# A decoder layer's FFN input: seven block products in place of eight for 19 of 22 steps

## The chip, the core and the metric

The kernel runs on one core of one Trainium2 chip. The metric is device time in microseconds (us) of one execution. The core has five engines with an instruction stream each, executed in order: PE (TensorE, matmuls; its weight loads appear as PEld), DVE (VectorE), ACT (ScalarE), POOL (GpSimd) and SP (SyncE, which here issues most transfers). They wait for one another through semaphores. On-chip memory is SBUF, with PSUM banks for the results of PE; a bank's tag in this kernel is one letter (g, s, t, d).

## The reference

One decoder layer for a prompt of 512 tokens with 16 meta tokens ahead of it, and for 8 samples of 8 tokens, of the same weights: differential attention and a gated delta rule (GDN) beside each other, their branches merged by gates, an output projection, then the gated FFN. The change concerns the FFN's first half:

```
xn = rmsnorm(x, p['ln_ffn_pre'])
up, gate = jnp.split(xn @ p['w_ffn_in'], 2, axis=-1)
gate, new_ffn_conv = causal_dwconv(gate, ffn_conv_buf, p['ffn_conv_w'], p['ffn_conv_b'])
x = x + rmsnorm((jax.nn.gelu(gate) * up) @ p['w_down'], p['ln_ffn_post'])
```

`xn` has 1024 features; `w_ffn_in` has 2 x 2816 columns; the convolution has width 3 along the tokens. The last two rows of `gate` before the convolution are outputs too (`new_ffn_conv`).

## The kernel before

Activations are held transposed, with features on the 128 partitions and tokens in the free dimension: 578 columns for the FFN (two meta tokens, 512 of the prompt, 64 of the samples). Products keep nearly the precision of float32: every operand is split into a rounded part `hi` (an ACT cast, L305) and the rest `lo` (a DVE subtraction, L306), and a product is three matmuls, hi by hi, hi by lo and lo by hi (L263). Weights come in tiles of 4 x 128 rows by 128 columns (512 elements a partition), loaded by SP into `wraw` (three buffers), two tiles for a column block.

The FFN input (`ffn_in`) walks 22 blocks m of 128 columns. A step makes the gate block g and the up block u: each eight blocks of 128 rows by three matmuls by two halves of the tokens (258 and 320 columns for g, 256 and 320 for u), 96 matmuls in all, in banks taken in turn. g is copied by ACT to `fpre` (L1656 to L1658); POOL puts the state rows ahead of it (L1655) and copies its last two rows to `ftail` (L1660, L1661). The convolution is one DVE tensor_scalar (L1665) and two DVE scalar_tensor_tensor (STT, L1669), each over 592 elements; gelu is on ACT (L1672). DVE multiplies by u out of PSUM (L1675 to L1677), and the product is split at once to `ghi` and `glo` (L1683, L1684) for the second half of the FFN, `ffn_out`. PE transposes `ftail` (L411), DVE copies it to `ftailT` (two buffers, L1688), and POOL's queue stores it (L1690, L1691).

The order of each engine is that of the program, with some reordering by a scheduler. Three half products are issued early (EARLY), since the last block of tokens is late. The convolution's constants and states, `fw`, are loaded by three DMAs on ACT's queue (L1622 to L1624) and transposed by PE in 22 pieces just after the first step's g; DVE copies them out (L1629). Ahead of the FFN stand `mix` and `out_proj`, whose `finish` normalises a block of tokens, transposes it (L411) and splits it into the FFN's input parts. Long before, the stage of the gates (`gate`, whose tanh is L1490) fills PE beside the last GDN head.

## Time and profile before

| | us |
|---|---|
| median of 3 runs | 1219.9 |
| lowest and highest run | 1218.33, 1222.36 |
| the profiled execution | 1219.77 |
| its span, first to last instruction | 1218.0 |
| granted TensorE clock, mean | 0.991 |
| a step of the FFN input (see the prediction) | 12.89 |

The profile is that of one execution. Its page gives the busy time of each engine, the groups of instructions by line of the kernel with their mean duration, and the chain of work that ended last. Other views of the same trace give busy time by stretch of time, the waits, the instructions of one line, and a timeline. In a timeline row the first number is the start, the second the duration, and xN counts instructions joined in a row; in a group's row the numbers after the bar are the busy time in us and the mean of one in ns. PE's matmuls overlap in the pipeline, so the spacing of starts, not the duration of one, is what a matmul costs; the same holds in part for DVE and ACT.

### The profile page before, as it was taken

The page shows a single profiled execution, that of the slowest core. Times are in us where ns is not written, and L with a number is a line of the kernel's source. Part 1 is how long each engine was busy: PE and PEld are TensorE (multiplying, and loading weights), DVE is VectorE, ACT ScalarE, POOL GpSimd, SP SyncE. Part 2 cuts the span into 40 slices and gives each one's busy share as a digit, 9 for nine tenths or more (in the row PEclk, how much of TensorE's full clock was granted, in tenths as well). Part 3 has the DMA queues.
Part 4 walks back from the last instruction along what each step waited for, and adds up shares of the span by engine and source line. Part 5 has one row for each costly group of instructions (what it writes and reads, how often), then busy time and mean ns, then how long its engine had stood idle before and what let it go on. Part 6 is the DMA issues. An engine that isn't in the chain of part 4 may idle for free.

```text
span 1218.0 us, 23729 instructions
## 1 busy us (share of the span) xinstructions
PE 1159.3 (95%) x8927; PEld 1036.0 (85%) x8927; DVE 638.2 (52%) x1719; ACT 447.3 (37%) x1139; POOL 206.5 (17%) x341
## 2 busy tenths in 40 slices
PE   6999999979999989899999999999999999999996
PEld 5977787757687677599998987899999999999996
DVE  5456667596487388346235753455545545422224
ACT  5234445443343243343233433433333333323322
POOL 2122221150241231221010002321111111100000
PEclk9999999999999999999999999999999999999999
DMA  6364525736936946713221552322223223352222
GB/s 197 77 237 133 160 64 180 238 113 201 302 108 192 300 154 192 252 47 86 69 70 55 149 163 87 102 81 85 75 86 88 84 75 88 95 166 79 79 80 85
DMA packets 185002, 157.57 MB, mean 129 GB/s; under 512 B 13234, under 2 KB 147315, under 8 KB 184867
## 3 DMA queue, kind: packets, MB, share of 16 engines
q1 hardware_dynamic: 179569, 147.53, 40.1%
q0 software_dynamic: 4288, 5.16, 1.5%
q10 hardware_dynamic: 1030, 3.35, 0.9%
q8 instruction: 71, 1.16, 0.4%
q14 instruction: 44, 0.36, 0.1%
HBM read 146.12 MB, written 9.88 MB: 128 GB/s over the span
## 4 chain that ended last, share of the span: by engine, by line
PE 69%; issue 13%; DVE 9%; POOL 3%; ACT 3%; DMA 2%; SPq 0%; DVEq 0%; ACTq 0%; POOLq 0%
PE ps_d L263 28%; PE ps_g L263 14%; PE ps_t L263 11%; PE ps_s L263 9%; PE ps_t L411 6%; DVE cy L639 1%; PE ps_m L263 1%; DVE KT L1393 1%; DMA page<-in_cache_k 1%; DMA page<-in_cache_v 1%; DVE vt L646 1%; DVE wlo L306 0%; DVE yn L1744 0%; POOL xr L406 0%; ACT whi L305 0%
## 5 line engine op out<-in xcount | busy, mean ns | idle before, releaser
L306 DVE TENSOR_TENSOR wlo<-wraw,whi 128x512 fp32r<-128x512 f32 x238 | 159.6, 684 | 243.6 <-ACT whi L305 241.9
L305 ACT CAST whi<-wraw 128x512 fp32r<-128x512 f32 x240 | 142.7, 613 | 253.9 <-PE ps_d L263 106.6
L263 PE MATMUL ps_d<-xhi,whi 128*128 128x256 f32 (+2 forms) x704 | 219.0, 311 | 0.0
L263 PE MATMUL ps_d<-xhi,wlo 128*128 128x256 f32 (+2 forms) x704 | 213.5, 304 | 1.2 <-DVE wlo L306 1.2
L263 PE MATMUL ps_d<-xlo,whi 128*128 128x256 f32 (+2 forms) x704 | 213.3, 303 | 0.3 <-DVE xlo L306 0.2
L263 PEld LDWEIGHTS ps_d<-xhi,whi 128*128 128x128 f32 x704 | 134.3, 191 | 7.4 <-issue 4.2
L263 PEld LDWEIGHTS ps_d<-xlo,whi 128*128 128x128 f32 x704 | 134.1, 190 | 3.6 <-issue 2.5
L263 PEld LDWEIGHTS ps_d<-xhi,wlo 128*128 128x128 f32 x704 | 133.8, 190 | 2.6 <-DVE wlo L306 1.6
L411 PE MATMUL ps_t<-consts,page 128*128 128x128 f32 x512 | 73.5, 283 | 8.9 <-DVE KT L1393 7.5
L411 PEld LDWEIGHTS ps_t<-consts,page 128*128 128x128 f32 x512 | 57.5, 143 | 25.5 <-issue 10.3
L263 PE MATMUL ps_t<-fhi,whi 128*128 128x320 f32 (+2 forms) x208 | 62.1, 299 | 0.1
L1393 ACT COPY KT<-ps_t 128x512 f32<-128x512 f32 x64 | 37.4, 585 | 65.5 <-PE ps_t L411 62.8
L263 PE MATMUL ps_t<-flo,whi 128*128 128x320 f32 (+2 forms) x208 | 61.3, 295 | 0.0
L263 PE MATMUL ps_t<-fhi,wlo 128*128 128x320 f32 (+2 forms) x208 | 61.1, 295 | 0.0
L263 PE MATMUL ps_g<-fhi,whi 128*128 128x320 f32 (+2 forms) x200 | 59.5, 298 | 0.0
L263 PE MATMUL ps_g<-flo,whi 128*128 128x320 f32 (+2 forms) x200 | 58.9, 295 | 0.0
L263 PE MATMUL ps_g<-fhi,wlo 128*128 128x320 f32 (+2 forms) x200 | 58.7, 294 | 0.0
L263 PE MATMUL ps_d<-fhi,whi 128*128 128x320 f32 (+2 forms) x192 | 57.4, 299 | 0.2 <-ACT fhi L305 0.2
L263 PE MATMUL ps_d<-flo,whi 128*128 128x320 f32 (+2 forms) x192 | 56.8, 296 | 0.0
L263 PE MATMUL ps_d<-fhi,wlo 128*128 128x320 f32 (+2 forms) x192 | 56.7, 296 | 0.0
L1393 DVE COPY KT<-ps_t 128x512 f32<-128x512 f32 x64 | 43.7, 685 | 18.1 <-PE ps_t L411 17.9
L263 PEld LDWEIGHTS ps_t<-fhi,whi 128*128 128x128 f32 x208 | 39.1, 188 | 0.7 <-ACT whi L305 0.3
(554 smaller groups left out, 2824.6 us busy)
## 6 DMA issues: line engine op xcount, KB each, us to landing
page<-in_cache_k SPq DMA_DIRECT2D x128, 256.0 KB, 4.1
page<-in_cache_v SPq DMA_DIRECT2D x128, 256.0 KB, 4.3
wraw<-in_w_in SPq DMA_DIRECT2D x88, 256.0 KB, 3.4
wraw<-in_w_ffn_in SPq DMA_DIRECT2D x88, 256.0 KB, 3.1
wraw<-in_w_down SPq DMA_DIRECT2D x40, 256.0 KB, 3.0
wraw<-in_w_out SPq DMA_DIRECT2D x16, 256.0 KB, 3.0
x<-in_x_prompt SPq DMA_DIRECT2D x4, 512.0 KB, 7.4
st<-in_state_gdn SPq DMA_DIRECT2D x4, 512.0 KB, 4.1
```

Of the source, the lines that this page charges most:

```text
L263: self.nc.tensor.matmul(out, lhsT, rhs, **kw)
L305: self.nc.scalar.copy(hi, raw)
L306: (eng or self.nc.vector).tensor_tensor(out=lo, in0=raw, in1=hi.bitcast(F32), op=ALU.subtract)
L411: self.nc.tensor.transpose(out, in_, self.ident[:k, :k])
L639: nc.vector.scalar_tensor_tensor(out=y, in0=pre[:, j : j + n], scalar=self.cw[:, ch, 24 + j : 25 + j], in1=y, op0=ALU.mult, op1=ALU.add)
L646: nc.vector.scalar_tensor_tensor(out=dst, in0=part(th), scalar=1.0, in1=part(y_), op0=ALU.add, op1=ALU.mult)
L1393: (nc.scalar.copy if j % 2 else nc.vector.tensor_copy)(kt[:, :, 128 * j : 128 * j + 128], tp)
```

## The change

Steps 0 to 2 stay as they are in kind, with token halves of equal width: the input is now held in four blocks `f["11"]`, `f["12"]`, `f["21"]`, `f["22"]`, the first index for the half of the features, the second for the half of the tokens, of 290 columns each (256 of the prompt, 32 of the samples, 2 for the meta tokens, zero in the second half). Steps 3 to 21 compute g and u together as the product of a 2 x 2 block matrix of weights (a11, a12 the two halves of g's rows; a21, a22 those of u) by the 2 x 2 blocks of f, with seven block products in place of eight (Winograd's form of Strassen's scheme). Each is 12 matmuls of 290 columns:

- weight sums: s1 = a21 + a22, s2 = s1 - a11, s3 = a11 - a21, s4 = a12 - s2. s1 and s3 are made on POOL, s2 and s4 on DVE. Each of s1 to s4 and a22 is split, beside g's two tiles: seven splits a step in place of four.
- input sums t1 to t4, made once by `differences` for each half of the feature blocks: five DVE and five POOL operations and four splits of 580 elements each time, during the plain steps.
- p1 and p2 give g's first half. In bank A (tag g) p1, p6, p7, p4 are accumulated on one another; ACT copies the bank after p1 (for g) and after p6 (`u2`), DVE reads it after p7 (into `p5`) and after p4 (u's first half). In bank C (tag t) p3 is accumulated on p5, after an ACT copy. The order on PE is p1, p5, p2, p6, p4 of the step before, its tail transpose, p3, p7, so that two products lie between a bank's copy and the next product into it.
- g's halves are summed into `fpre` by DVE (`add_g`), the convolution's first operation moves from DVE to ACT (Identity with scale and bias), u's second half is multiplied on POOL, its first half on DVE.
- u's weights have buffers of their own, `raw`, three for two tiles a step.
- the product `gf` is kept whole, in the buffers of the gates (tag gt) and four of a pool gx; seven are split ahead of the last p4, fifteen in `ffn_out`.
- `ftailT` has one buffer, its copy moves to ACT, and the tail's transpose always goes to the bank with tag s.
- `ffn_consts` moves to the stage of the gates, ahead of the first gate, with 18 loads on ACT's queue into six tiles of the gates' buffers.
- a constant of 0.5 (`phalf`) becomes a small tile where it is used.

The diff, cut to its core:

```diff
-EARLY = (("g", 0), ("u", 0), ("g", 1))
+NC = 290
+PLAIN = 3
...
+                        self.ffn_consts()
...
-            self.f = self.parts(fx, "f", 8, HALF_G)
+            self.f = {
+                key: tuple(self.t(fx, [128, 4, NC], f"f{p}{key}", F32R) for p in ("hi", "lo")) for key in ("11", "12", "21", "22")
+            }
+            for key in ("12", "22"):
+                for e in self.f[key]:
+                    nc.scalar.copy(e[:, :, 288:290], self.c("zero").unsqueeze(2).to_broadcast([128, 4, 2]))
             with ExitStack() as s:
                 self.out_proj(self.pool(s, "wout"), wo0)
...
+    def put_f(self, g, half, c, p):
+
+        hi, lo = self.f[f"{g + 1}{half + 1}"]
+        self.split(hi[:, :, c], lo[:, :, c], p)
+
+    def differences(self, gx, e):
+
+        f = self.f
+        k = slice(2 * e, 2 * e + 2)
+        (h11, l11), (h12, l12), (h21, l21), (h22, l22) = (
+            (u[:, k].bitcast(F32) for u in f[key]) for key in ("11", "12", "21", "22")
+        )
+        r1, r2, r3, r4 = (
+            self.t(gx, [128, 2 * NC], f"gf{NF - 4 + j}").rearrange("p (k c) -> p k c", k=2) for j in range(4)
+        )
+        v, g = self.nc.vector, self.nc.gpsimd
+
+        def op(eng, out, a, b, o=ALU.subtract):
+            eng.tensor_tensor(out=out, in0=a, in1=b, op=o)
+
+        def part(j, r):
+            hi, lo = (u[:, k] for u in f[f"t{j}"])
+            self.split(hi, lo, r)
+
+        op(v, r1, h12, h11)
+        op(g, r3, h22, h12)
+        op(v, r1, r1, l11)
+        op(v, r1, r1, l12, ALU.add)
+        op(g, r3, r3, l22, ALU.add)
+        op(v, r2, h22, r1)
+        op(v, r2, r2, l22, ALU.add)
+        op(g, r3, r3, l12)
+        part(1, r1)
+        part(2, r2)
+        op(g, r4, h21, r2)
+        op(g, r4, r4, l21, ALU.add)
+        part(3, r3)
+        part(4, r4)
...
+    def ffn_consts(self):
         nc, a = self.nc, self.a
-        nat = self.t(tmp, [20, DFF], "fnat")
-        nc.scalar.dma_start(nat[:16], a["state_ffn_conv"][0].rearrange("b j c -> (b j) c"))
-        nc.scalar.dma_start(nat[16:19], a["ffn_conv_w"][0])
-        nc.scalar.dma_start(nat[19:20], a["ffn_conv_b"])
-        fw = self.t(pool, [128, NF, 20], "fw")
+        self.fw = fw = self.t(self.gtpool, [128, NF, 20], "fw", bufs=1)
         p = self.ps("t")[:, : NF * 20].rearrange("p (k c) -> p k c", k=NF)
-        for k in range(NF):
-            self.transpose(p[:, k], nat[:, 128 * k : 128 * k + 128])
+        for k0 in range(0, NF, 4):
+            n = min(4, NF - k0)
+            nat = self.t(self.gtpool, [128, NQ], "gt", bufs=18)[:, : 128 * n]
+            sl = slice(128 * k0, 128 * (k0 + n))
+            nc.scalar.dma_start(nat[:16], a["state_ffn_conv"][0].rearrange("b j c -> (b j) c")[:, sl])
+            nc.scalar.dma_start(nat[16:19], a["ffn_conv_w"][0][:, sl])
+            nc.scalar.dma_start(nat[19:20], a["ffn_conv_b"][:, sl])
+            for k in range(n):
+                self.transpose(p[:, k0 + k], nat[:20, 128 * k : 128 * k + 128])
         nc.vector.tensor_copy(fw, p)
...
+        def load_u(st):
+            raw = []
+            for k in (0, 512):
+                t = self.t(w7, [128, 4, 128], "raw", bufs=3)
+                nc.sync.dma_start(
+                    t, w[k : k + 512, 128 * st["m"] : 128 * st["m"] + 128].rearrange("(k p) c -> p k c", p=128)
+                )
+                raw.append(t)
+            st["rawu"] = raw
+
+        def combine(st, key, x, y, op, eng=nc.gpsimd):
+            t = self.t(w7, [128, 4, 128], "sw", bufs=3)
+            eng.tensor_tensor(out=t, in0=x, in1=y, op=op)
+            st["r" + key] = t
+
+        def divide(st, key, src=None):
+            hi, lo = (self.t(w7, [128, 4, 128], tag, F32R, bufs=n) for tag, n in (("hw", 7), ("lw", 6)))
+            self.split(hi, lo, st["r" + key] if src is None else src)
+            st[key] = four(hi, lo)
+
+        def weights_s(st):
+            (a11, a12), (a21, a22) = st["raw"], st["rawu"]
+            combine(st, "s1", a21, a22, ALU.add)
+            combine(st, "s2", st["rs1"], a11, ALU.subtract, nc.vector)
+            divide(st, "s1")
+            combine(st, "s4", a12, st["rs2"], ALU.subtract, nc.vector)
+            divide(st, "s2")
+            divide(st, "s4")
+
+        def weights_r(st):
+            (a11, a12), (a21, a22) = st["raw"], st["rawu"]
+            combine(st, "s3", a11, a21, ALU.subtract)
+            divide(st, "s3")
+            divide(st, "22", a22)
+
+        def product(ps, wt, x, first):
+            hi, lo = wt
+            xhi, xlo = x
+            for k in range(4):
+                kw = {} if first else {"skip_group_check": True}
+                self.mm(ps, hi[k], xhi[:, k], start=first and k == 0, stop=False, **kw)
+                self.mm(ps, hi[k], xlo[:, k], start=False, stop=False, **kw)
+                self.mm(ps, lo[k], xhi[:, k], start=False, stop=k == 3, **kw)
+
+        def saved(ps, tag):
+            t = self.t(pool, [128, NC], tag, bufs=2 if tag == "p5" else 1)
+            nc.scalar.copy(t, ps)
+            return t
...
+            sv = pre[:, 514:].rearrange("p (b j) -> p b j", b=NB)
+            nc.vector.tensor_tensor(
+                out=pre[:, 256 * half + 2 : 256 * half + 258], in0=ps[:, 0:256], in1=t[:, 0:256], op=ALU.add
+            )
+            if half == 0:
+                nc.vector.tensor_tensor(out=pre[:, 0:2], in0=ps[:, 288:290], in1=t[:, 288:290], op=ALU.add)
+            ss = lambda u: u[:, 256:288].rearrange("p (b t) -> p b t", b=4)
+            nc.vector.tensor_tensor(out=sv[:, 4 * half : 4 * half + 4, 2:10], in0=ss(ps), in1=ss(t), op=ALU.add)
...
+        def p1(st):
+            begin(st)
+            st["A"] = self.ps("g")[:, :NC]
+            product(st["A"], st["11"], f["11"], True)
+            st["p1"] = saved(st["A"], "p1")
+
+        def p2(st):
+            ps = self.ps("d")[:, :NC]
+            product(ps, st["12"], f["21"], True)
+            add_g(st, 0, ps, st["p1"])
+
+        def p3(st):
+            product(st["C"], st["s4"], f["22"], False)
+
+        def p5(st):
+            st["C"] = self.ps("t")[:, :NC]
+            product(st["C"], st["s1"], f["t1"], True)
+            st["p5"] = saved(st["C"], "p5")
+
+        def p6(st):
+            product(st["A"], st["s2"], f["t2"], False)
+            st["u2"] = saved(st["A"], "u2")
...
-            nc.vector.tensor_scalar(
-                y, pre[:, 0:n], fw[:, m, 16:17], fw[:, m, 19:20], op0=ALU.mult, op1=ALU.add
-            )
+            nc.scalar.activation(y, pre[:, 0:n], AF.Identity, bias=fw[:, m, 19:20], scale=fw[:, m, 16:17])
...
+        def times(eng, st, half, u):
+            if gfs[st["m"]] is None:
+                gfs[st["m"]] = self.t(gx, [128, 2 * NC], f"gf{st['m']}")
+            gf, y_ = gfs[st["m"]], st["y"]
+            sl = slice(256 * half, 256 * half + 256)
+            eng.tensor_tensor(out=gf[:, sl], in0=y_[:, sl], in1=u[:, 0:256], op=ALU.mult)
+            eng.tensor_tensor(
+                out=gf[:, 512 + 32 * half : 544 + 32 * half].rearrange("p (b t) -> p b t", b=4),
+                in0=_strided(y_, 514, 10, TS)[:, 4 * half : 4 * half + 4],
+                in1=u[:, 256:288].rearrange("p (b t) -> p b t", b=4),
                 op=ALU.mult,
             )
-            nc.scalar.copy(ghi[m], gf)
-            nc.vector.tensor_tensor(out=glo[m], in0=gf, in1=ghi[m].bitcast(F32), op=ALU.subtract)
-            tp = self.ps("t")
-            self.transpose(tp[:18, :128], tail)
-            rows = self.t(pool, [18, 128], "ftailT", bufs=2)
-            nc.vector.tensor_copy(rows, tp[:18, :128])
+
+        def p7(st):
+            product(st["A"], st["s3"], f["t3"], False)
+            nc.vector.tensor_tensor(out=st["p5"], in0=st["A"], in1=st["p5"], op=ALU.add)
+            times(nc.gpsimd, st, 1, st["p5"])
+
+        def p4(st):
+            product(st["A"], st["22"], f["t4"], False)
+            times(nc.vector, st, 0, st["A"])
+            store(st)
+
+        def store(st):
+            m = st["m"]
+            tp = self.ps("s")
+            self.transpose(tp[:18, :128], st["tail"])
+            rows = self.t(pool, [18, 128], "ftailT", bufs=1)
+            nc.scalar.copy(rows, tp[:18, :128])
             sl = slice(128 * m, 128 * m + 128)
             nc.gpsimd.dma_start(o["new_ffn_conv_prompt"][0, 0, :, sl], rows[0:2])
             nc.gpsimd.dma_start(o["new_ffn_conv_sample"][0, :, :, sl].rearrange("b j c -> (b j) c"), rows[2:18])
...
+            ps = self.psd()[:, : NC - 2 * half]
+            plain(ps, st["wg"], half, NC - 2 * half)
...
+        sts = [{"m": m} for m in range(PLAIN)]
+        plain_g(sts[0], 0)
+        plain_u(sts[0], 0)
+        plain_g(sts[1], 0)
+        plain_g(sts[0], 1)
+        conv(sts[0])
+        plain_u(sts[0], 1)
+        plain_end(sts[0])
+        self.differences(gx, 0)
+        plain_g(sts[1], 1)
+        conv(sts[1])
+        for half in range(2):
+            plain_u(sts[1], half)
+        plain_end(sts[1])
+        self.differences(gx, 1)
+        for st in sts[2:]:
+            for half in range(2):
+                plain_g(st, half)
+            conv(st)
+            for half in range(2):
+                plain_u(st, half)
+            plain_end(st)
+        nxt = weights_g(PLAIN)
+        load_u(nxt)
+        weights_s(nxt)
+        weights_r(nxt)
+        last = None
+        for m in range(PLAIN, NF):
+            st = nxt
+            p1(st)
+            p5(st)
+            p2(st)
+            if m + 1 < NF:
+                nxt = weights_g(m + 1)
+                load_u(nxt)
+            p6(st)
+            if last:
+                p4(last)
+            if m + 1 < NF:
+                weights_s(nxt)
+            p3(st)
+            add_g(st, 1, st["C"], st["u2"])
+            conv(st)
+            p7(st)
+            if m + 1 < NF:
+                weights_r(nxt)
+            last = st
+        self.gf, self.gx, self.ghi, self.glo, self.room = gfs, gx, [], [], []
+        for p, j in (("hi", 1), ("lo", 1), ("hi", 2), ("lo", 2)):
+            self.make_room(p, j)
+        for m in range(7):
+            self.divide_gf(m)
+        p4(last)
```

More of the change, by code (lines that the diff above doesn't have):

```diff
@@ L519, in gdn_scalars @@
         sqb = tmp("sqb")
+        half = tmp("half")
+        nc.vector.memset(half, 0.5)
         nc.gpsimd.tensor_tensor(
-            out=sqb, in0=beta, in1=self.phalf[:, : nch * H].rearrange("p (c h) -> p c h", h=H), op=ALU.pow
+            out=sqb, in0=beta, in1=half, op=ALU.pow
         )
@@ L1691, in ffn_in, with plain @@
             nc.gpsimd.dma_start(o["new_ffn_conv_sample"][0, :, :, sl].rearrange("b j c -> (b j) c"), rows[2:18])
-    def ffn_out(self, pool, w3, ghi, glo):
-        nc, a, o = self.nc, self.a, self.o
+        def plain(ps, w, half, n):
+            his, los = w
+            for k in range(8):
+                xhi, xlo = (u[:, k % 4, :n] for u in f[f"{k // 4 + 1}{half + 1}"])
+                self.mm(ps, his[k], xhi, start=k == 0, stop=False)
+                self.mm(ps, his[k], xlo, start=False, stop=False)
+                self.mm(ps, los[k], xhi, start=False, stop=k == 7)
@@ new lines, in plain_w, with plain_g @@
+        def plain_w(c0, m):
+            if m != 1:
+                return self.weight(w, c0 + 128 * m)
+            his, los = [], []
+            for raw in self.raw_w(w, c0 + 128 * m):
+                hi, lo = (self.t(w7, [128, 4, 128], tag, F32R, bufs=n) for tag, n in (("hw", 7), ("lw", 6)))
+                self.split(hi, lo, raw)
+                his += [hi[:, k] for k in range(4)]
+                los += [lo[:, k] for k in range(4)]
+            return his, los
+        def plain_g(st, half):
+            if not half:
+                st["wg"] = plain_w(DFF, st["m"])
+                begin(st)
+            ps = self.psd()[:, : NC - 2 * half]
+            plain(ps, st["wg"], half, NC - 2 * half)
+            pre = st["pre"]
+            sv = pre[:, 514:].rearrange("p (b j) -> p b j", b=NB)
+            nc.scalar.copy(pre[:, 256 * half + 2 : 256 * half + 258], ps[:, 0:256])
+            nc.scalar.copy(
+                sv[:, 4 * half : 4 * half + 4, 2:10], ps[:, 256:288].rearrange("p (b t) -> p b t", b=4)
+            )
+            if not half:
+                nc.scalar.copy(pre[:, 0:2], ps[:, 288:290])
@@ new lines, in plain_u, with plain_end @@
+        def plain_u(st, half):
+            if not half:
+                st["wu"] = plain_w(0, st["m"])
+            st["u", half] = self.psd()[:, :288]
+            plain(st["u", half], st["wu"], half, 288)
+        def plain_end(st):
+            for half in range(2):
+                times(nc.vector, st, half, st.pop(("u", half)))
+            store(st)
+        sts = [{"m": m} for m in range(PLAIN)]
[3 more added lines that the diff above has]
+        plain_g(sts[0], 1)
@@ new lines, in ffn_in @@
+        conv(sts[0])
[9 more added lines that the diff above has]
+        for st in sts[2:]:
+            for half in range(2):
+                plain_g(st, half)
+            conv(st)
+            for half in range(2):
+                plain_u(st, half)
+            plain_end(st)
```

119 lines of the change are left out of this document (64 added, 55 removed).

## The prediction

> **What bounds the kernel now.** I read the page first for the engines' shares, then the table of busy time by stretch for the FFN input, then the chain of waits for the length of a step, and last the groups of instructions for prices.
>
> ```profile
> span 1218.0 us, 23729 instructions
> PE 1159.3 (95%) x8927; PEld 1036.0 (85%) x8927; DVE 638.2 (52%) x1719; ACT 447.3 (37%) x1139; POOL 206.5 (17%) x341
> 520.00:530.00 10.00, 10.00 (x74) 9.40 (x74) 3.10 (x8) 2.37 (x7) 1.07 (x1) 1.00 0.03 8
> 850.00:900.00 50.00, 50.00 (x377) 49.77 (x376) 24.11 (x46) 16.35 (x34) 6.54 (x18) 1.00 0.30 86
> 900.00:950.00 50.00, 50.00 (x379) 49.77 (x378) 25.64 (x48) 16.65 (x36) 7.10 (x20) 1.00 0.30 86
> ```
>
> PE is busy for the whole of the FFN input at a granted clock of 1.00 (in the rows of 50 us PE is busy for 50.00, and the third column from the end is the clock), with DVE half used, ACT a third, POOL a seventh. The gate stage near 520 us is just as full. So PE's columns set the time, and any wait put before PE in either place is lost whole.
>
> ```profile
> 795.17 1.67 PE ps_t L411 x23
> 812.04 3.52 PE ps_d L263 x24
> 815.56 0.11 PE ps_t L411
> 815.67 2.90 PE ps_d L263 x24
> 824.94 3.51 PE ps_s L263 x24
> 828.45 0.11 PE ps_t L411
> ```
>
> These pieces of the chain are matmuls on end. From one tail transpose (815.56) to the next (828.45) a step takes 12.89 us, so 19 steps take 244.9. Twenty-four matmuls of 258 columns take 2.90 (0.1208 each), of 320 columns 3.52 (0.1467): 0.417 ns a column, and a 290-column matmul is 0.134 by interpolation.
>
> **The change part by part: PE.** Nineteen steps go from 96 matmuls to 84 of 290 columns: 84 x 0.134 + 0.11 = 11.4 us. If PE alone set the pace, this would be 1.5 us a step, 28.7 in all. The three plain steps keep their 1154 columns for each weight tile, so they change nothing on PE.
>
> **What is added beside PE.**
>
> ```profile
> L306 DVE TENSOR_TENSOR wlo<-wraw,whi 128x512 fp32r<-128x512 f32 x81 | 53.6, 679 | 86.0 <-ACT whi L305 86.0
> L305 ACT CAST whi<-wraw 128x512 fp32r<-128x512 f32 x80 | 47.8, 621 | 87.6 <-PE ps_g L263 26.2 <-PE ps_d L263 24.3 <-PE ps_t L263 22.5
> L1669 DVE SCALAR_TENSOR_TENSOR fy<-fpre,fw,fy 128x592 f32<-128x592 f32 x43 | 35.5, 829 | 0.7
> L1672 ACT ACTIVATE fy<-fy 128x592 f32<-128x592 f32 x22 | 15.4, 699 | 55.5 <-DVE fy L1669 55.5
> L1660 POOL COPY ftail<-fpre 128x2 f32<-128x2 f32 x20 | 8.7, 435 | 107.5 <-ACT fpre L1657 107.5
> L1661 POOL COPY ftail<-fpre 128x16 f32<-128x16 f32 x21 | 4.7, 223 | 0.0
> L1676 DVE TENSOR_TENSOR fgf<-fy,ps_d 128x256 f32<-128x256 f32 x7 | 2.9, 418 | 7.2 <-PE ps_d L263 7.2
> L1656 ACT COPY fpre<-ps_g 128x258 f32<-128x258 f32 x6 | 2.3, 377 | 8.7 <-PE ps_g L263 8.7
> 927.54 1.70 DVE L1669 SCALAR_TENSOR_TENSOR fy<-fpre,fw,fy 128x592 f32<-128x592 f32 x2
> 932.31 1.27 DVE L306 TENSOR_TENSOR wlo<-wraw,whi 128x512 fp32r<-128x512 f32 x2
> L379 POOL TENSOR_TENSOR y<-xr,lnf 128x512 f32<-128x512 f32 x4 | 5.2, 1293 | 0.3
> L306 POOL TENSOR_TENSOR wlo<-wraw,whi 128x512 fp32r<-128x512 f32 x2 | 2.5, 1273 | 1.3 <-ACT whi L305 1.3
> L952 POOL TENSOR_TENSOR lbt<-dtbig_low,consts x4: 351/354/900, 263.6 to 553.4; 80x80 f32<-80x80 f32 x4
> wraw<-in_w_ffn_in SPq DMA_DIRECT2D x68, 256.0 KB, 3.0
> out_new_ffn_conv_prompt<-ftailT POOLq DMA_DIRECT2D x17, 1.0 KB, 1.6
> out_new_ffn_conv_sample<-ftailT POOLq DMA_DIRECT2D x17, 8.0 KB, 3.1
> ```
>
> Two splits back to back take 1.27, so a 512-element DVE operation costs about 0.6 in a row and a 592-element one 0.85. On POOL 512 elements cost 1.28 and 80 cost 0.354 (the rows above), so by the line between them 256 cost 0.74, 32 cost 0.25, 580 cost 1.44. Per step DVE gets nine operations of 512 (seven splits, s2, s4) 5.4, two of 592 1.7, the sums of g about 1.0, p7's sum 0.4, half of the product with u 0.5: 9.0 us. ACT gets about 7 (seven casts, Identity, gelu, three copies), POOL 4.5 (s1 and s3 2.55, its half of the product 1.0, the tail copies 0.65, the state rows 0.25). Each fits under 11.4, so by busy time all of it is hidden by PE. The steps at which engines wait for one another do not.
>
> **The loop.** By the order of the changed kernel's instructions, gelu of step m-1 leads to gelu of step m: POOL's half product 1.0; s3 1.27 behind it on POOL; the `raw` slot (three for two tiles a step) that s3 frees, then the load of a22 two steps on, 3.0 and its issue 0.1; s1 on POOL 1.27; s2 on DVE 0.6, which waits for s1 while everything of step m queues behind it; g's second half 0.45; a split 0.6 and s4 0.6 (Identity runs beside them on ACT); STT 0.85; p7's sum 0.4; STT 0.85; gelu 0.7. That is 11.7. Seven hand-overs between engines at 0.05 or so make 12.1: already over PE's 11.4. PE is tied to it, since p7's bank is freed by the u2 copy, which stands behind the previous gelu on ACT, and p4's and the next p1's by DVE operations behind it.
>
> ```profile
> 338.10 0.85 DVE L639 SCALAR_TENSOR_TENSOR cy<-pre,cw,cy 128x616 f32<-128x616 f32 x1
> 338.26 1.87 POOL L739 TENSOR_TENSOR dbig_low<-dd,consts 128x512 f32<-128x512 f32 x1 [5.89 <-DVE dd L736]
> 338.87 1.29 DVE L743 COPY elast<-er 128x4 f32<-128x4 f32 x1
> 531.98 0.16 DVE L743 COPY elast<-er 128x4 f32<-128x4 f32 x1
> 532.13 1.29 POOL L739 TENSOR_TENSOR dbig_low<-dd,consts 128x512 f32<-128x512 f32 x1 [11.07 <-DVE elast L743]
> 532.24 1.27 DVE L802 TENSOR_TENSOR er<-q,er 128x64 f32<-128x64 f32 x1
> L802 DVE TENSOR_TENSOR er<-q,er x4: 202/216/1270, 245.8 to 532.2; 128x64 f32<-128x64 f32 x4
> ```
>
> POOL and DVE also stop each other: a DVE sum of 64 elements takes 0.216 by its median but 1.27 under POOL's operation at 532.13, and POOL's operation at 338.26 takes 1.87 in place of 1.29 because DVE's was running. A step has 7.1 us of DVE operations with both inputs in SBUF and 4.4 of POOL's; most are off the loop and can meet it. The Trainium skill, "SBUF — State Buffer", section "Who interferes with whom", states the same as a rule: a DVE instruction with two SBUF inputs and a GpSimd instruction that reads SBUF exclude each other for a whole instruction. By that rule this change, which puts both kinds into each step, pays twice for engines that look idle; the rows agree. I take one such meeting of 0.6 a step: 12.7 (bounds 11.7, none and no hand-over, and 13.4, two meetings). The first two steps find their weights ready, and p6's bank is left alone for two products (3.2 us less its copy's 0.38, so about 3 of slack). So 2 x 11.4 + 17 x 12.7 - 3 = 235.7, or 9.2 less than 244.9; bounds -26 and +3.
>
> **The plain steps.** The page of before has no `differences`. Gelu of step 0 now stands on ACT behind casts that need nine POOL sums of 1.44 or 1.27 and two tail copies: 13.5 us in one row, starting about 3 us after the last block is transposed. Then two casts, gelu (0.7) and the product: about 20 when nothing meets. PE has five half tiles, 5 x 24 x 0.134 = 16.1, and then stands at step 0's tail transpose, since that transpose uses bank s, which the product must empty: 4 us lost. Meanwhile DVE has some fourteen two-input operations of 0.6 to 0.85; where each of nine POOL sums waits for one, 0.45 on average, another 4 are lost: 8 (bounds 2 and 12). What hid this before is that gelu waited for nothing but its convolution. Then `ftailT`, now one buffer, waits for its store to land (3.1, row above): PE's next half tile in bank s is about 1 to 2 late, and no less than nothing. I take 9, bounds 2 and 14.
>
> **The constants.** They leave 1.67 us of transposes (795.17) in the FFN.
>
> ```profile
> L1622 ACTq DMA_DIRECT2D fnat<-in_state_ffn_conv x1: 332/332/332, 780.4 to 780.4; - x1
> DMA to landing us min/median/max: 3.4/3.4/3.4
> 517.02 0.39 ACT L1490 ACTIVATE gt<-ps_d 128x256 f32<-128x256 f32 x1
> 518.56 0.36 PE L263 MATMUL ps_d<-xhi,whi 128*128 128x256 f32 x1
> ```
>
> In the gate stage they become 18 small loads on ACT's queue ahead of the first gate's tanh (517.02), and five of six tiles' transposes stand ahead of the next gate matmul (518.56) on PE. At 0.33 an issue and 3.4 to land, with the ninth load waiting for the first, the fifth tile's last one lands about 526: 7.6 lost; behind the sixth tile a little more. PE is full from 520 on, so nothing hides it. Were each to land as fast as the 1 KB stores, in 1.6, issue alone would set it: 517.1 + 15 x 0.33 + 1.6 = 523.7, 5.1 lost; if the scan beside it has slack, 2. Net of 1.67: +6, bounds 0 and +7.
>
> **End.** Seven parts are split before the last p4: 0.6 on DVE against PE's 3.2 for two products; I take +0.5, bounds 0 and 2. Out-projection splits and the `half` constant are on no path: 0.
>
> **Sum.** -9.2 + 9 + 6 + 0.5 = +6.3. The profiled execution took 1219.8 (1.8 around its span), as the median of the runs, so 1226; I say 1225, as the port meetings that I charged may overlap the stalls.
>
> **The rivals.** (1) PE sets the pace in all 19 steps: loads run further ahead than I read, -28.7, with 9 to 15 of stalls: 1200 to 1207. For it: all engines' sums lie under 11.4. Against: the loop alone is over it. (2) The loop at 12.2 cancels the stalls: 17 x 12.2 + 19.8 = 227.2, -17.7 + 15.5 = -2: 1218, no change. (3) The port decides: at 13.4 or more the loop itself is slower than before (+2.7), which with the stalls as taken is 1238, and with those of the plain steps at 14, 1243. The turning point is a step of 13.2 for the loop alone (17 x 13.2 + 19.8 = 244.2) and of 12.3 with the 15.5 of stalls. (4) The products don't shorten PE because a 290-column matmul in an alternating bank is no shorter in proportion: then 12.9 stays and 15 is added, 1235; the 258 and 320 rows on one line speak against it.
>
> **How the numbers follow.** Forecast (1219 to 1233) 0.48, of which 0.05 within the bound; rival 1, 0.17; rival 2, 0.15, of which 0.09 is no change and 0.06 faster; rival 3, 0.17; rival 4, 0.03. A measurement here tells 0.3% (3.7 us) from no change. Faster 0.23, no change 0.14, slower 0.63. The range 1203 to 1241 leaves out the tips of rivals 1 and 3; the forecast's own is 1219 to 1233.
>
> **What would show it.** Right: step period near 12.7 between tail transposes; PE idle before p7 or p4, released by ACT's u2 copy or DVE; SP's `raw` loads waiting for POOL's s3; DVE's s2 idle behind POOL; an idle of 6 to 8 before the first gate matmuls after 518; 8 or more idle at step 0's tail transpose. Wrong: PE full at 11.4 a step, or gate matmuls between the constants' loads.

## The result, and the profile after

The changed kernel takes 1226.34 us in the median of 5 runs (1225.42 to 1231.11), the kernel before 1218.36 (1217.47 to 1222.36, 5 runs): a ratio of 1.0068, 95% interval 1.005 to 1.0086. It is slower, by about 8 us; the forecast was 1225, in a range of 1203 to 1241. The profiled execution is the highest of the five, 1231.11, and its span 1229.4; what of that belongs to that execution alone is taken out below.

A line of the page of the changed kernel (busy time of each engine, its share of the span, and its instructions):

```profile
PE 1151.9 (94%) x8699; PEld 1019.2 (83%) x8699; DVE 741.3 (60%) x1888; ACT 505.5 (41%) x1260; POOL 307.2 (25%) x427
```

228 matmuls are gone (8927 to 8699) and PE is busy 7.4 us less, while DVE has 103 more and POOL 101 more. The work did move from PE to the other engines; the time did not follow.

Where it went is read from a few landmarks in the order of PE. Rows of PE's timeline before, and then after (start, duration, line, operation, and in brackets the idle time before it):

```profile
779.27 1.06 PE L411 MATMUL ps_t<-consts,y 128*128 128x128 f32 x8 [1.19 <-DVE y L395]
...
815.40 0.27 PE L411 MATMUL ps_t<-consts,ftail 128*18 128x128 f32 x1
...
1060.37 0.27 PE L411 MATMUL ps_t<-consts,ftail 128*18 128x128 f32 x1
```

```profile
792.47 1.06 PE L421 MATMUL ps_t<-consts,y 128*128 128x128 f32 x8 [0.54 <-DVE y L405]
...
819.96 0.37 PE L421 MATMUL ps_s<-consts,ftail 128*18 128x128 f32 x1 [10.64 <-POOL ftail L1793]
...
820.37 0.44 PE L273 MATMUL ps_g<-fhi,hw 128*128 128x288 f32 x1
820.61 0.44 PE L273 MATMUL ps_g<-flo,hw 128*128 128x288 f32 x1
...
839.93 0.27 PE L421 MATMUL ps_s<-consts,ftail 128*18 128x128 f32 x1
...
908.12 0.27 PE L421 MATMUL ps_s<-consts,ftail 128*18 128x128 f32 x1
...
1054.08 0.27 PE L421 MATMUL ps_s<-consts,ftail 128*18 128x128 f32 x1
...
1069.77 0.28 PE L421 MATMUL ps_s<-consts,ftail 128*18 128x128 f32 x1 [0.56 <-POOL ftail L1793]
...
1070.93 0.29 PE L273 MATMUL ps_g<-fhit,hw 128*128 128x290 f32 x1
```

The first row of each is the last block's transposes, where the FFN begins; the row at 815.40 or 839.93 is the tail transpose of step 2, with which the plain part ends; the row at 1060.37 or 1069.77 is that of step 21. In the changed kernel, the last product p4 of step 21 stands behind that transpose: its twelve matmuls begin at 1070.93, 1.6 us in all. Before, nothing of step 21 stands there. From these rows, in the profiled executions:

| stretch | before | after | difference | forecast |
|---|---|---|---|---|
| start to the FFN | 779.27 | 792.47 | +13.2 | +7.6 (constants, gross) |
| plain steps, with the constants' transposes before | 36.13 | 47.46 | +11.3 | +9, less 1.67 |
| 19 steps, to the tail transpose of step 21 | 244.97 | 229.84 | -15.1 | |
| p4 of step 21 behind it | 0 | 1.6 | +1.6 | -9.2, with the row above |
| the rest of the span | 157.6 | 158.0 | +0.4 | +0.5 |
| sum | 1218.0 | 1229.4 | +11.4 | +6.3 |

So the 19 steps as a whole take 231.4 and save 13.5.

Of the 13.2, 5.5 arose ahead of the constants and in this execution alone. PE's matmuls that read the paged cache stood at 488.25 before and at 487.90 after; the last of them at 513.43 and at 518.98. From these last ones to the FFN are 265.84 and 273.49, and the 7.65 between the two are what the constants' new place adds. In the 5.5 lies a stretch with a low granted clock (columns of the table by stretch: length, PE, PEld, DVE, ACT, POOL busy, clock, DMA share, GB/s), first of before, then of after:

```profile
505.00:510.00 5.00, 4.46 (x34) 2.42 (x30) 2.28 (x5) 0.72 (x3) 0.00 (x0) 1.00 0.96 304
```

```profile
505.00:510.00 5.00, 4.46 (x25) 2.67 (x18) 0.90 (x3) 0.63 (x3) 0.00 (x0) 0.50 0.88 270
525.00:530.00 5.00, 3.61 (x24) 3.14 (x24) 0.21 (x2) 1.23 (x5) 0.37 (x1) 0.50 0.17 46
810.00:815.00 5.00, 0.00 (x0) 0.00 (x0) 5.00 (x5) 0.18 (x1) 4.84 (x4) 0.87 0.00 0
```

The first row of after is the one that the change does not touch: in the traces of the ten kernels of the experiments, this stretch has a clock of 1.00, and the last of the paged-cache matmuls stands between 511.45 and 515.89. The other two are stalls of the change. Where before had PE full at a clock of 1.00 (the prediction's row of 520 to 530), PE has 24 matmuls in 5 us, at half the clock. The rows of ACT there show why (ACTq is its queue of transfers):

```profile
522.57 0.33 ACTq L1668 DMA_DIRECT2D gt<-in_state_ffn_conv  x1
...
528.65 0.76 ACT L1502 ACTIVATE gt<-ps_d 128x256 f32<-128x256 f32 x2 [5.98 <-DMA gt<-in_ffn_conv_w]
```

Eighteen issues like the first stand in one row up to 528.60, 0.335 each, and the first tanh of the gates comes behind all of them: 6.1 us after the first issue. It is 11.6 later than in the kernel before (517.02), the other 5.5 being the delay that is older than the constants. PE's transposes of the tiles wait for the loads, and the first gate matmul follows them at 529.42, 5.3 later than before (518.56) when the delay is taken off. Then 17 gate matmuls follow at 0.21 each, where the later ones take 0.12: 1.6 more.

The stretch of 810 to 815 is the stall at step 0's tail transpose: no matmul in 5 us, while DVE is busy for 5.00 with five instructions and POOL for 4.84 with four. The largest of POOL's groups between 793 and 830, and then rows of ACT's timeline:

```profile
L1638 POOL TENSOR_TENSOR gf<-gf,flo 128x580 f32<-128x580 f32 x6 | 11.0, 1838 | 0.4
```

```profile
816.06 0.68 ACT L315 CAST fhit<-gf 128x580 fp32r<-128x580 f32 x1 [5.88 <-POOL gf L1638]
...
818.57 0.70 ACT L1802 ACTIVATE fy<-fy 128x592 f32<-128x592 f32 x1
```

Gelu of step 0 stands in ACT's order behind a cast that waits 5.88 us for POOL's input sums. Its own convolution on DVE, between the input sums there, ends at 814.76, 1.3 before that cast begins, so the cast is what held it last. Behind the cast come a second one and a table load of ACT (1.28 at 817.27) ahead of gelu; in the kernel before, the same load ran at 795.70, in a wait for the convolution, and cost nothing. The row of POOL's group has six of the input sums at 1.84 each (the four others are at 1.93), where the line through the rows of before gave 1.44. With gelu, the product, the bank, and with it PE's transpose are late.

Then the 19 steps. One lap of the chain of waits (start, duration, what; short pieces are left out):

```profile
870.34 0.99 POOL gt L1810
...
871.54 1.27 POOL sw L1711
872.83 2.88 DMA raw<-in_w_ffn_in
...
875.94 1.29 POOL sw L1711
...
877.28 0.57 issue
877.86 0.42 DVE fpre L1751
...
878.37 0.61 DVE lw L316
879.01 0.69 DVE sw L1711
879.70 0.74 DVE fy L1799
...
880.73 0.83 DVE fy L1799
...
882.38 0.99 POOL gt L1810
```

POOL's half product, s3, the load into the buffer that s3 frees, s1, s2, g's second half, a split, s4, the convolution, p7's sum, convolution, then gelu (0.70 on ACT from 881.59, which the view shows as a POOL copy in its shadow), and the half product again (the 0.57 called issue is s2 on DVE): 12.04 us, piece for piece the loop of the prediction. PE's tail transposes come every 11.42 us from 862.45 to 908.12, and from there to 1054.08 twelve periods take 145.96, or 12.16 each. The waits (who waited, for what: us in total, times, longest) show the same loop from the side of the loads on SP's queue, and two waits of PE for the `u2` copy, which the prediction named as a sign but did not price:

```profile
PE ps_g L273 <- ACT u L1745: 3.4, 2, 2.6
...
SPq L1703 <- POOL sw L1711: 35.4, 16, 2.5
```

The longer of the two is in step 3, ahead of the loop. ACT's copy stands there behind a cast that waits for a load of g's weights; rows of ACT and of PE:

```profile
849.63 0.62 ACT L315 CAST whi<-wraw 128x512 fp32r<-128x512 f32 x1 [2.54 <-DMA wraw<-in_w_ffn_in]
...
851.12 0.49 PE L273 MATMUL ps_g<-fhit,hw 128*128 128x290 f32 x1 [2.61 <-ACT u L1745]
```

The shorter (0.79 at 1044.30) lies within the twelve periods.

### The profile page after: what moved, and what is told of

The parts are those of the page before. It is cut to its first block, busy times and chain, and to the rows that moved or that the text cites. A ratio compares the mean times of both kernels' runs of the same rounds, so it can differ in the third digit from the quotient of the medians.

```text
span 1229.4 us, 23799 instructions
## 1 busy us (share of the span) xinstructions
PE 1151.9 (94%) x8699; PEld 1019.2 (83%) x8699; DVE 741.3 (60%) x1888; ACT 505.5 (41%) x1260; POOL 307.2 (25%) x427
## 5 line engine op out<-in xcount | busy, mean ns | idle before, releaser
L315 ACT CAST whi<-wraw 128x512 fp32r<-128x512 f32 x198 | 116.9, 611 | 163.2 <-PE ps_d L273 86.4
L273 PE MATMUL ps_g<-fhit,hw 128*128 128x290 f32 x228 | 69.6, 305 | 4.5 <-ACT u L1745 3.4
L273 PE MATMUL ps_g<-flot,hw 128*128 128x290 f32 x228 | 68.1, 299 | 0.0
L273 PE MATMUL ps_g<-fhit,lw 128*128 128x290 f32 x228 | 67.8, 297 | 0.0
L316 DVE TENSOR_TENSOR lw<-sw,hw 128x512 fp32r<-128x512 f32 x76 | 54.0, 711 | 0.3 <-ACT fy L1802 0.2
L315 ACT CAST hw<-sw 128x512 fp32r<-128x512 f32 x76 | 46.6, 613 | 7.6 <-DVE sw L1711 5.0
L273 PEld LDWEIGHTS ps_g<-fhit,hw 128*128 128x128 f32 x228 | 43.4, 190 | 6.9 <-ACT u L1745 3.9
L273 PEld LDWEIGHTS ps_g<-flot,hw 128*128 128x128 f32 x228 | 43.7, 192 | 0.0
L273 PEld LDWEIGHTS ps_g<-fhit,lw 128*128 128x128 f32 x228 | 43.7, 191 | 0.0
L273 PE MATMUL ps_s<-KT,qb 128*32 128x256 f32 x512 | 38.4, 402 | 1.4 <-DVE KT L1405 1.1
```

The source lines that it names most:

```text
L273: self.nc.tensor.matmul(out, lhsT, rhs, **kw)
L315: self.nc.scalar.copy(hi, raw)
L316: (eng or self.nc.vector).tensor_tensor(out=lo, in0=raw, in1=hi.bitcast(F32), op=ALU.subtract)
```

## The experiments

Each kernel was run against the kernel before on the same chip; the ratios are to it, with a 95% interval. The changed kernel itself has 1.0068. The medians of before lay between 1217.64 and 1220.73 from chip to chip, so a difference between two changed kernels can hold a part of that; the ratios are free of it.

**A fourth buffer for u's weights.** Every fourth tile goes into a tile that is free until the last step's product.

```diff
-                t = self.t(w7, [128, 4, 128], "raw", bufs=3)
+                i = 2 * (st["m"] - PLAIN) + k // 512
+                if i % 4 < 3 or st["m"] > 18:
+                    t = self.t(w7, [128, 4, 128], "raw", bufs=3)
+                else:
+                    t = self.t(gx, [128, 2 * NC], f"gf{NF - 1}")[:, :512].rearrange("p (k c) -> p k c", k=4)
```

> The changed kernel with a fourth buffer for u's raw weights (every fourth tile lies in a tile of pool gx that is not needed before step 19). The load of a22 then waits no longer for s3 of the step before, so the chain gelu, half product, s3, load, s1, s2, s4, gelu is open. If that chain sets the period of 12.07 us between tail transposes, the period falls to PE's own 11.4 and the time by 7 to 13 us against the changed kernel's 1226, to 1213 to 1219. If the port that POOL and DVE share sets it (the same operations are left), the period stays within 0.2 of 12.07 and the time at 1224 to 1228.

Measured: 1214.78, ratio 0.9967 (0.9955 to 0.9979). From 899.92 to 928 its chain of waits holds nothing but PE:

```profile
902.73 0.11 PE ps_s L421
...
904.46 3.23 PE ps_g L273 x24
...
914.15 0.11 PE ps_s L421
```

The tail transposes come every 11.42 from step 3 to step 20, and the stretch from that of step 2 to that of step 21 takes 219.56, 10.3 less than with three buffers. The operations on DVE and POOL are the same, and they still hold each other up (DVE's split of g's weights takes 1.035 on the mean, where 0.68 is usual), so what held the step at 12.16 was the buffer, not the port or an engine's load.

**The product with u on DVE alone.**

```diff
-            times(nc.gpsimd, st, 1, st["p5"])
+            times(nc.vector, st, 1, st["p5"])
```

> The changed kernel with u's second half multiplied on DVE instead of POOL. It takes POOL's 1.25 us (256 and 32 elements) out of the chain and s3 out from behind gelu, and adds about 0.55 us a step to DVE's own work of 9.0. If the chain sets the period, it falls to 11.4 to 11.6 and the time by 6 to 12 us, to 1214 to 1220. If DVE's or the port's load sets it, the period grows to 12.2 to 12.6: 1226 to 1232.

Measured: 1226.0, ratio 1.0059 (1.0038 to 1.0079): a miss, nothing gained. The half product is gone from POOL, but twelve periods from 900.52 on take 12.2 each, and the chain shows a loop with another first part:

```profile
910.49 0.71 ACT fy L1802
...
911.75 0.61 DVE lw L316
...
912.49 1.31 POOL sw L1711
...
913.81 2.89 DMA raw<-in_w_ffn_in
...
924.58 1.31 POOL sw L1711
```

s3 takes one of three `sw` buffers, and the one that it takes is freed by a split on DVE that now stands behind gelu's product. From s3 to s3 are 12.09 us. The load, s1 and all that follows are as before.

**A buffer of its own for s3**, on top of the last edit.

```diff
-            t = self.t(w7, [128, 4, 128], "sw", bufs=3)
+            if key == "s3" and st["m"] < 18:
+                t = self.t(gx, [128, 2 * NC], f"gf{NF - 2}")[:, :512].rearrange("p (k c) -> p k c", k=4)
+            else:
+                t = self.t(w7, [128, 4, 128], "sw", bufs=3)
```

> The changed kernel with u's second half multiplied on DVE (as e2_product_dve) and besides a buffer of its own for s3 (in a tile of pool gx not needed before step 18). In e2_product_dve the chain ran on, closed by another wait: s3 took the buffer of s1, which the split of s1 on DVE, behind gelu's product, frees. If that is so, s3 now comes early, the period falls from 12.07 to 11.4 and the time to 1214 to 1220. If not the chain but the load on DVE and the port sets the period, it stays at 12.0 or more: 1224 to 1230.

Measured: 1223.6, ratio 1.0049 (1.003 to 1.0069): a second miss. POOL's timeline shows how the loop closed a third time:

```profile
946.22 0.68 POOL L1795 COPY ftail<-fpre 128x2 f32<-128x2 f32 x1 [2.52 <-DVE fpre L1754]
...
947.00 1.30 POOL L1714 TENSOR_TENSOR gf<-wraw,raw 128x512 f32<-128x512 f32 x1
...
958.31 0.68 POOL L1795 COPY ftail<-fpre 128x2 f32<-128x2 f32 x1 [2.53 <-DVE fpre L1754]
```

s3 (the row at 947.00) now stands behind the tail copies in POOL's order; these wait for g's second half, which on DVE stands behind s2 and so behind s1 and the load; 12.09 from 946.22 to 958.31. Near the end, where the edit gives s3 one of the `sw` buffers again, the last four periods are 11.41 to 11.44. The three kernels have one piece in common, from s3 by its freed buffer to the load and s1. Only the fourth buffer took it out.

**The input sums later.** The scheduler is told to place `differences` behind other work, with the sums themselves unchanged.

```diff
-        self.differences(gx, 0)
+        with self.tc.high_priority(offset=-400):
+            self.differences(gx, 0)
...
-        self.differences(gx, 1)
+        with self.tc.high_priority(offset=-400):
+            self.differences(gx, 1)
```

> The changed kernel with the input sums (differences) at a lower priority: three of the nine POOL sums that ACT's casts wait for ahead of gelu of step 0 move behind it. If that row of POOL sums is what holds PE at step 0's tail transpose (10.6 us), three sums of 1.9 us and a cast less leave 4 to 6, and the time falls by 4 to 6 us, to 1220 to 1222. If something else holds the bank (the table load, u's second half), or the sums come back as a wait ahead of p5 of step 3, the time stays within 2 us of 1226.

Measured: 1221.46, ratio 1.0023 (1.0012 to 1.0034). PE's waits:

```profile
PE ps_s L421 <- DVE gt L1811: 6.0, 1, 6.0
PE ps_s L273 <- ACT ftailT L1833: 3.7, 1, 3.7
```

The stall at step 0's tail went from 10.6 to 6.0, but 3.7 came back at the next product into bank s, and the plain steps take 47.62 as they did (47.46). What was gained lies in the 19 steps, 225.1 in place of 229.8, where the wait for `u` in step 3 fell from 2.6 to 0.8. So the time is in the range that was expected, but not for the reason expected: putting the sums off moves the stall within the plain steps, and the gain came behind them.

**The input sums on DVE alone.**

```diff
-        v, g = self.nc.vector, self.nc.gpsimd
+        v, g = self.nc.vector, self.nc.vector
```

> The changed kernel with all ten sums of each call of differences on DVE, none on POOL. On POOL one took 1.9 us beside DVE's work (1.44 by the line from undisturbed rows), on DVE 0.68. If the port that the two share is what fills the plain steps (from the last block's transposes to step 2's tail transpose 47.5 us, against 36.1 before), 14 to 19 us of POOL's time become 7 of DVE's, PE's wait at step 0's tail transpose falls from 10.6 to 2 to 6 us, the stretch to 39 to 44 us and the time by 4 to 9 us, to 1217 to 1222. If DVE itself is the limit there, it gets worse by the 7 us: 1230 to 1234.

Measured: 1217.42, ratio 1.0 (0.9987 to 1.0012), 8.9 us under the changed kernel. DVE does ten sums in place of five each time, and yet the stall at step 0's tail is gone. One wait is left:

```profile
PE ps_s L273 <- DVE wlo L316: 5.6, 1, 5.6
```

The plain steps take 43.98, 3.5 less, and the 19 steps 224.2, 5.7 less, since the wait in step 3 is gone too. The work shared out over two engines was slower than all of it on one of them. Two things changed at once: each of DVE's sums takes 0.69 to 0.76 here, where in the changed kernel they took between 0.75 and 2.00, and the row of POOL's sums, at 1.8 to 2.0 each, is gone. By the prediction's line POOL's would be slower than DVE's (1.44) with nothing beside them, so how much of the gain is POOL's own pace and how much the two engines' holding each other up was not told apart.

**The constants' transposes later.** The 18 loads go on SP's queue at the same place, the transposes behind the third gate.

```diff
-                        self.ffn_consts()
+                        self.ffn_consts_load()
                         for i in range(16):
                             yield from self.gate(i)
+                            if i == 2:
+                                self.ffn_consts()
...
-            nc.scalar.dma_start(nat[:16], a["state_ffn_conv"][0].rearrange("b j c -> (b j) c")[:, sl])
+            nc.sync.dma_start(nat[:16], a["state_ffn_conv"][0].rearrange("b j c -> (b j) c")[:, sl])
...
```

> The changed kernel with the constants' 18 loads on SP's queue in place of ACT's, and their 22 transposes after the third gate in place of ahead of the first, among gate matmuls. If PE's stand in the gate stage costs what the trace shows (529.4 against 518.6 for the same matmul, of which 5.9 was there before it, and a lower clock for a few us after), the time falls by 5 to 8 us, to 1218 to 1221. If the scan beside it had slack, so that the stand was filled later, by 0 to 2: 1224 to 1226.

Measured: 1231.91, ratio 1.0109 (1.0086 to 1.0131): a clear miss. The gates' tanh in this kernel:

```profile
L1504 ACT ACTIVATE gt<-ps_d x32: 362/408/442, 531.4 to 665.6; 128x256 f32<-128x256 f32 x16, 128x322 f32<-128x322 f32 x16
```

The first comes at 531.4, 20.0 behind the last paged-cache matmul (511.45); in the changed kernel 9.7 and before 3.6. SP issued the 18 loads from 514.1 to 520.6, ahead of the gates' weights, which it also loads. PE's waits between 518 and 536 show none for a load; the longest is 4.4, for ACT's part of a GDN step (`gjunk`). So it was the order of the work there, and not a late load, that held the gates back; how the loads' new queue led to that order was not followed.

**The constants spread out.** On ACT's queue again, but one tile's three loads behind each of the first six gates, and the transposes behind the ninth.

```diff
-                        self.ffn_consts()
+                        self.nats = []
                         for i in range(16):
+                            if 0 < i < 7:
+                                self.ffn_consts_load(i - 1)
                             yield from self.gate(i)
+                            if i == 8:
+                                self.ffn_consts()
```

> The changed kernel with the constants' loads still on ACT's queue, but three (one tile) after each of the first six gates, and the transposes after the ninth gate. e3_consts_later moved 18 loads to SP's queue and was 5.6 us slower than the changed kernel; my account of that is that the loads held up SP, which brings the gates' weights, so that PE had nothing between the steps of the scan. If that account holds, nothing holds PE now and the time falls by 6 to 9 us below the changed kernel's 1226, to 1217 to 1220. If the later place of the transposes made e3 slow, the time stays at 1226 or above.

Measured: 1217.61, ratio 0.9997 (0.9983 to 1.001): 8.7 us under the changed kernel. The FFN begins at 778.51 (before 779.27), and the stretch in dispute is full again, although the transposes stand later still than in the last kernel, so their later place was not what made that one slow:

```profile
520.00:530.00 10.00, 10.00 (x73) 9.40 (x72) 3.39 (x8) 2.51 (x7) 0.80 (x1) 1.00 0.05 12
```

**The three together**: fourth buffer, input sums on DVE, constants spread.

> The changed kernel with the three edits together: the fourth raw buffer (e1_raw4, measured 1214.8), the constants spread (e5_consts_spread) and the sums on DVE (e7_sums_dve). If their costs lie in different stages, the gains add up: 1214.8 less 6 to 9 less 4 to 9, so 1197 to 1205, below both kernels. If one of the two new ones fails, 1205 to 1212; if the raw buffer's gain came from slack that the other stalls gave, above 1212.

Measured: 1201.36, ratio 0.9866 (0.9847 to 0.9885). The gains of the three alone are 11.6, 8.9 and 8.7 against 1226.34, 29.2 in all; together they give 25.0, with the 5.6 us wait for `wlo` still there. From the tail transpose of step 2 to that of step 21 it takes 215.8, and with the p4 behind it 217.4, close to PE's pace as the prediction reckoned it (244.9 - 28.7 = 216.2). This version beats both kernels.

**Two attempts at that last wait**: the input sums on DVE put off by 400 as well, and four plain steps in place of three (`PLAIN = 4`).

> e8_combined with the input sums at a lower priority besides. In e8 PE still waits 5.6 us in the plain steps, for the split of step 2's weights on DVE, which stands behind the sums of both calls; here it stands ahead of most of them. If that wait is only a matter of DVE's order, it goes and the time falls by 3 to 6 us, to 1195 to 1198. If DVE as a whole is full in the plain steps, the wait comes back ahead of p5 or p3 of step 3, and the time stays at 1200 to 1203.

> e8_combined with four plain steps and 18 steps of seven products. One step more at 12.89 in place of 11.4 costs 1.5 us. If the plain steps are full because DVE's sums don't fit beside three of them, PE's waits there (5.6 and 0.8) shrink by 3 or more, and the time falls by 1 to 4 us, to 1197 to 1200. If the wait is where DVE's order puts the split of step 2's weights, it stays, and the time grows to 1202 to 1204.

Measured: 1202.41 (ratio 0.9854, 0.9832 to 0.9877) and 1204.54 (0.9882, 0.9854 to 0.9909). By the ratios, neither is told from the combined kernel. With the sums put off, the 5.6 is gone, and the plain steps take 36.13, as before the change; but the first steps of seven products get slower, with waits of up to 1.3, and the 19 steps take 222.8 in place of 215.8. With a fourth plain step the 5.6 stays and one more step is made of eight products.

## Why the prediction was right

The sum came out at +6.3 and the medians differ by 8.0. Without the 5.5 of that one execution, its span grew by 5.9. The mechanisms were the ones named, but that the sum fits so well is in part luck: the 19 steps came out 4.3 better than forecast, the plain steps 4.0 worse, and in the constants two errors cancelled.

- **The loop.** Right in its pieces and its length: 11.7 of work and 12.1 with hand-overs were forecast, and the lap measures 12.04. The experiment with a fourth buffer shows that it is a loop through the buffer and nothing else. What was mis-sized is the 0.6 for one meeting of POOL and DVE on it: no piece of the lap shows one of that size (the largest excess is the half product, 1.20 for a forecast 1.0). Against 12.7 the 12.16 saves 17 x 0.54 = 9.2, so the forecast's sum gives 226.5 in place of 235.7. What it didn't have is the wait for `u` in step 3: 2.6, then fifteen matmuls at 0.24 in place of 0.134, 1.6 more. A last 0.6 is the wait at the tail transpose of step 21. That is 231.3 for a measured 231.4, so the lead of PE at the start, two steps and 3 us, agrees; it shows as the periods of 11.42 up to 908.12.
- **The plain steps.** The place and the chain were right: gelu on ACT behind casts that wait for POOL's sums, and PE at step 0's tail transpose. So was the size of the meetings: POOL's sums took 0.40 to 0.49 over the line, for a forecast 0.45 on average. The stall was 10.6 for a forecast 8; the chain left out the table load of 1.28 ahead of gelu. Another consequence was missing. After the stall, PE's matmuls stand 0.24 apart (820.37, 820.61) and not 0.134, for some fifteen of them: 1.6 more. `ftailT` with one buffer cost 0.3, not 1 to 2. Against the 34.5 of before without the constants' transposes, the stretch grew by 13.0 for a forecast 9.
- **The constants.** The 7.65 less the 1.67 of transposes is 6.0, for a forecast 6. In the five other kernels with the constants where the change put them, the way from the last paged-cache matmul to the FFN is 6.4 to 8.0 longer than before, 4.7 to 6.4 net. Spreading them out brought it back to 265.36 and bought 8.7 in the median. But the terms were others. The forecast had 7.6 up to the first gate matmul, with 3.4 from issue to landing and the ninth load waiting for the first. The fifth tile's last load was issued at 527.34 and its transposes came at 528.90, so it landed in 1.6 or less, and that matmul was 5.3 late, which is the prediction's lower case (5.1). No load waited in this execution; with the fourth buffer the eighth was issued 3.4 us after the first, and the matmul was 6.35 late. The rest came from the low clock afterwards, which the forecast did not have.
- **The end.** +0.4 for a forecast 0.5, once p4 of step 21 is counted with its step.
- **The rivals.** The first, PE's pace in all steps, and the third, the port deciding the loop at 13.4, both fall by the measured period; a 290-column matmul does take its share (84 and a transpose in 11.42, forecast 11.4), so the fourth falls too. The second had the loop at 12.2, which is nearly what was measured, but made 227.2 of the 19 steps where they took 231.4, and paired it with stalls of 15.5 where 13.0, 6.0 and 0.4 are 19.4. In the length of the step it was nearer than the forecast.

So the forecast was right in that it charged the stalls that come once, at the seams, against a gain that the loop had already cut. With the seams as written, even taking the loop away gave no more than 1214.78.

## What to carry to other kernels

An engine that looks idle by its share can still be part of a loop: where a step frees the buffer into which the same stage's weights are loaded, add the durations around that loop and compare the sum with the bound engine's step, before work is moved there. Take away the edge (here one more buffer), not a piece: two edits that took pieces out let the loop close by another way at nearly the same length. And price the seams by themselves: eighteen small loads in one row on a queue whose engine the full stage needs cost as much as all of the saving of six steps.

## What the hardware showed unexpectedly

**The clock after a stall.** A stall of PE can cost more than its idle time. After 10.6 us without a matmul the table by stretch of the changed kernel reads:

```profile
815.00:820.00 5.00, 0.04 (x2) 0.07 (x2) 4.39 (x7) 3.91 (x7) 2.03 (x4) 0.50 0.01 3
```

and the matmuls come 0.24 us apart up to 823.97, then 0.134 again: 4 us at half pace. The Trainium skill, "TensorE: Matmul & The Clock Gate", section "Part 1: The HAM clock gate", states that PE goes to half rate after an idle window of about 3.4 us and back after about as long a busy one. The stall of 10.6 and the 4 us behind it agree. The wait in step 3 does not quite: there 2.6 us of idle were enough, and the matmuls come 0.24 apart from 851.12 to 854.76. The low clock of 505 to 510 in the one execution came with PE busy for 4.46 of 5.00; no row here shows its cause.

**DVE and POOL hold each other up.** In the stall of 810 to 815 both DVE and POOL are busy to the brim, yet finish only five and four instructions. Two sums of 580 elements in DVE's timeline of the changed kernel, the first beside POOL's sums and the second with POOL idle:

```profile
814.69 1.96 DVE L1638 TENSOR_TENSOR gf<-gf,flo 128x580 f32<-128x580 f32 x1
...
820.16 0.75 DVE L1638 TENSOR_TENSOR gf<-fhi,gf 128x580 f32<-128x580 f32 x1
```

In the 19 steps the same shows off the loop; DVE's groups of the changed kernel from 860 to 1050:

```profile
L316 DVE TENSOR_TENSOR lw<-sw,hw 128x512 fp32r<-128x512 f32 x63 | 43.0, 682 | 0.0
L316 DVE TENSOR_TENSOR wlo<-wraw,whi 128x512 fp32r<-128x512 f32 x32 | 36.8, 1189 | 5.6 <-ACT whi L315 5.5
```

The same subtraction of the same size takes 0.682 in one place of the step and 1.189 in another. The second kind runs in pairs that begin while POOL makes s3: at 883.65 a pair takes 2.34, and s3 ends at 884.84. In the kernel with a buffer of its own for s3, which stands elsewhere in POOL's order, the same subtraction takes 0.747 on the mean, and POOL's s1 1.51 in place of 1.29: the meeting has moved there. In the changed kernel the half a microsecond, twice a step, is paid by DVE's slack; DVE is busy for 10.08 of the 12.07 us from 870.34 on.
